# Three spacer tiles wider by 128 bytes: dense products whose operands and weights all begin at 64 modulo 256 bytes

## The chip, the core and the metric

The kernel runs on one NeuronCore of a Trainium2 chip. The metric is the device time of one execution in microseconds (us). Times of several executions are given as a median with the lowest and the highest; the profile is of one further execution.

## What is computed

A two-layer encoder trunk over 1280 tokens of 1024 channels, float32. The tokens are two batches that share the weights: a prompt of 256 and a sample of 1024. Layer 0 mixes tokens with a bidirectional RWKV-7 recurrence, layer 1 with neighbourhood attention; after each mixer comes a squared-ReLU MLP.

```python
for layer in range(DEPTH):                       # 2
    h = _rms_norm(x, p['norm_mix_g'][layer])
    y = rwkv7_mixer(h, ...) if layer == 0 else neighbourhood_attention(h, ...)
    x = x + y                                    # y ends in "@ w_o", 1024 x 1024
    h = _rms_norm(x, p['norm_mlp_g'][layer])
    x = x + jnp.square(jax.nn.relu(h @ w_up[layer])) @ w_down[layer]   # 1024 -> 4096 -> 1024
```

## The kernel before

Activations lie channels by tokens: 8 blocks (`k`, `KT = 8`) of 128 channels on the 128 partitions, the tokens along the free dimension. The tokens come in three segments, `SEGS = [(0, 256), (256, 768), (768, 1280)]`: `s = 0` is the prompt, `s = 1, 2` are the sample, 512 columns each.

**Dense products.** A float32 operand is split into two `float32r` tiles, a high part and a low rest (`wsplit`, L93 to L104, for weights: ACT copies the high part, L102, another engine subtracts, L103). `mm3` (L106 to L110) then makes three TensorE products into one PSUM bank: high weights with high operand (L108), high weights with low operand (L109), low weights with high operand (L110). The weights are the stationary operand, 128 x 128, loaded before each product; the activations are the moving operand, 256 or 512 columns of 4 bytes.

**The two channel layers.** `channel_layer` (L1349 on) runs once for each layer: the mixer's output product with the residual, then the MLP. Its operand is `self.act`, made by `act_tiles` (L1223) in the pool `actp`: for each `k` a high and a low tile of the prompt (`ahp`, `alp`, 256 columns) and of the sample (`ahs`, `als`, 1024 columns). `dense` (L1385) runs over the 8 `k`, 24 matmuls for one bank. In the MLP the hidden layer has 32 blocks `f`. `up(f, s)` is one `dense` with the weights `whi`, `wlo` from the pool `clw`, then ReLU (L1439, ACT), square (L1440, POOL), and the split into `hh`, `hl` (L1442 ACT, L1443 DVE) in the pool `clh`. `down([f], s)` multiplies `hh`, `hl` with the weights of block `f` from the pool `cld`, 8 output blocks `m` of three matmuls each, and DVE adds each bank to `x` (L1461). The loop interleaves them: `up(f, 0)`, `down(f-1, 0)`, `up(f, 1)`, `down(f-1, 1)`, `up(f, 2)`, `down(f-1, 2)`. The order of the instructions is that of the code; the down products of the last two blocks come together at the end, in an order fixed by `manual_schedule`.

Between the layers `attention` runs with an order written out by hand for TensorE: query and key projections (`qk_proj`, weights in the pool `atw`, operand `self.act`), eight pairs of heads, scores, softmax, transposes against the identity in `cst`, values. Ahead of layer 0's channel layer `gated` makes the gate product (`sgh`, `sgl`, `sgs` with `gh`, `gl`, `gs`, four matmuls to a bank, the fourth with 96 rows) from tiles in the pool `gp`, which `gate_begin` opens while the recurrence is still running, together with layer 0's `clk` and `clw`. In the first part of the kernel the key projection multiplies `mh`, `ml` with `whi`, `wlo` (pools `mixp`, `wpA`), and the receptance product `rps` multiplies `mh`, `ml` with `wh`, `wl`.

**Where tiles lie.** Pools of the left side are stacked upward from the low end of a partition, in the order in which they are opened, those of the right side downward from the high end; inside a pool the tiles follow each other upward. So a tile's start is the sum of what lies before it. Some tiles in the code hold nothing: the ones named `space`, `space0`, `space1` only move what is laid behind them. Starts of the dense products' operands in the kernel before, in bytes modulo 256 (all columns and blocks that a product addresses begin a multiple of 256 bytes further, so the remainder holds for each of its reads):

| product | moving operand | start mod 256 | weights | start mod 256 |
|---|---|---|---|---|
| layer 0 output, up (sample) | `ahs`, `als` | 192 | `clw` | 192 |
| layer 0 down (sample) | `hh`, `hl` | 64 | `cld` | 192 |
| layer 1 output, up (sample) | `ahs`, `als` | 192 | `clw`, `atw` | 64 |
| layer 1 down (sample) | `hh`, `hl` | 64 | `cld` | 192 |
| query, key (sample) | `ahs`, `als` | 192 | `atw` | 64 |
| output, up, query, key (prompt) | `ahp`, `alp` | 96 | as the sample's | |
| down (prompt) | `hh`, `hl` | 224 | `cld` | 192 |
| gate product | `sgh`, `sgl`, `sgs` | 192 | `gp` | 192 |
| key projection of layer 0 | `mh`, `ml` | 64 | `wpA` | 64 |
| receptance product of layer 0 | `mh`, `ml` | 64 | `wh`, `wl` | 64 |

Modulo 512, `ahs` lies at 448, layer 0's `clw` at 192, layer 1's at 320, `hh` at 64, `cld` at 448, the gate's tiles at 192, `mh` at 64, `wpA` at 320, `wh` at 64.

Of the kernel before, what the change touches and what calls it, by code (L numbers as in the profile page):

```python
# [5 lines left out]
F32 = mybir.dt.float32  # L6
# [7 lines left out]
P = 128  # L14
# [47 lines left out]
class Trunk:  # L62
# [748 lines left out]
    def at(self, t, f, level=3):  # L811
        self.todo.append((t, len(self.todo), f, level))
# [410 lines left out]
    def act_tiles(self, pool):  # L1223
        
        def tiles(part, n):
            return [[pool.tile([P, n], F32R, name=f"{x}{part}{k}") for x in ("ah", "al")] for k in range(KT)]
        prompt = tiles("p", TP)
        pool.tile([P, 24], F32, name="space")
        sample = tiles("s", T - TP)
        return [tuple(Parts(p, s) for p, s in zip(prompt[k], sample[k])) for k in range(KT)]  # L1230

# [47 lines left out]
    def gate_begin(self):  # L1279


        nc, tc = self.nc, self.tc
        at = lambda t, f, *x: self.at(16.0 * (len(self.jobs) - 1) + t, lambda: f(*x))

        def begin():
            self.ectx.close()
            self.clctx, self.gctx = ExitStack(), ExitStack()
            pool = lambda c, name, bufs: c.enter_context(tc.tile_pool(name=name, bufs=bufs, reuse_waits="tile", side="right"))
            self.clk, self.clw = pool(self.clctx, "clk", 2), pool(self.clctx, "clw", 2)
            gp = self.gp = pool(self.gctx, "gp", 1)  # L1290
            self.gate = [[gp.tile([P if i < 2 else 96, n], F32R, name=nm + "hls"[i]) for i in range(3)] for nm, n in (("sg", T), ("g", 1024))]
            gp.tile([P, 512], F32, name="graw", tag="graw", bufs=7)
            self.wo = []

        def load(src, c0, c1, stacked):
            raw = self.gp.tile([P, 512], F32, name="graw", tag="graw", bufs=7)
            raw = raw[:, :c1 - c0]
            if stacked:
                for j in range(3):
                    nc.sync.dma_start(raw[32 * j:32 * j + 32], src[P:P + 32, c0:c1])  # L1300
            else:
                nc.sync.dma_start(raw, src[:P, c0:c1])
            self.graws.append(raw)

        def cut(i, c0, c1, stacked):
            raw = self.graws.pop(0)
            hi, lo, st = (z[:, c0:c1] for z in self.gate[i])
            if stacked:
                low = slice(32, 64) if i else slice(64, 96)
                nc.scalar.copy(st, raw[:96])  # L1310
                nc.gpsimd.tensor_tensor(out=st[low], in0=raw[low], in1=st[low].bitcast(F32), op=ALU.subtract)
            else:
                nc.scalar.copy(hi, raw)
                nc.gpsimd.tensor_tensor(out=lo, in0=raw, in1=hi.bitcast(F32), op=ALU.subtract)

        def weight(m):
            self.wo.append(self.wsplit(self.clw, self.a["w_o"][m], 1024, nc.gpsimd, tag="u"))
        self.graws = []
        at(2.0, begin)
        parts = [(i, c0, min(c0 + 512, n), st) for i, n in ((0, T), (1, 1024)) for st in (0, 1) for c0 in range(0, n, 512)]  # L1320
        for k, (i, c0, c1, st) in enumerate(parts):
            src = self.a["g2"] if i else self.scr["sg2_d"]
            t = 7.0 + 0.9 * k
            at(t - 2.0, load, src, c0, c1, st)
            at(t, cut, i, c0, c1, st)
        at(16.5, weight, 0)
        at(17.5, weight, 1)
# [21 lines left out]
    def channel_layer(self, layer, x_src, src, wname, dst, gnext=None, gate=False):  # L1349
# [6 lines left out]
        with ExitStack() as ctx:  # L1356
            pool = lambda name, side="left": ctx.enter_context(tc.tile_pool(name=name, bufs=2, reuse_waits="tile", side=side))
# [19 lines left out]
            wd_, wh_ = pool("cld"), pool("clh")  # L1377
            wh_.tile([P, 8], F32, name="space0", bufs=1)
            for t in ("hh", "hl"):
                wh_.tile([P, TP], F32R, name=t, tag=t + "False", bufs=2)  # L1380
            wh_.tile([P, 24], F32, name="space1", bufs=1)
            ones = xp.tile([P, P], F32, name="ones", bufs=1)
            nc.gpsimd.memset(ones, 1.0)

# [615 lines left out]
```

## Time and profile before

| | |
|---|---|
| median of 3 runs | 4114.17 us (4107.8 to 4115.26) |
| the profiled execution | 4116.18 us |
| its span, first to last instruction | 4114.4 us |
| mean granted TensorE clock | 0.961 of full speed |
| DMA | 393.22 MB, mean 96 GB/s |

The engines are PE (TensorE's matmuls), PEld (its loads of weights, beside the matmuls), DVE, ACT, POOL and SP, whose queue issues most DMAs. The row of an engine in the slices gives its busy share in each of 40 equal parts of the span, in tenths. A row of a group reads: line, engine, operation, output and inputs by the program's names with buffer numbers left out, shapes, count, then busy time and mean duration of one, then the time that the engine stood idle just before. A row of the timeline begins with the start of an instruction and its duration, both in us. The ends of matmuls are modelled and overlap, so that the pace of a stream is read from start to start.

In the span, layer 0's channel layer takes about 1424 to 2500 us with its MLP from about 1558 on, the attention about 2580 to 3095 us, layer 1's channel layer the rest, with its MLP from about 3230 on.

### The profile page before, as it was taken

Reading aid. Unit: us, or ns where it says so; the run is one execution under the profiler, and the core shown is the slowest. Engines: PE = TensorE matmul, PEld = TensorE weight load, DVE = VectorE, ACT = ScalarE, POOL = GpSimd, SP = SyncE. Lnnn points to the kernel's source line nnn. Section 1 sums busy time; section 2 is a strip of 40 time slices with the busy share of each in tenths; the row PEclk is TensorE's granted clock in tenths of the full one; section 3 lists DMA queues with packets and bytes.
Section 4 is the critical chain, followed back from the end, with each engine's and each line's share of the span. In section 5 each row is a group of like instructions: output and inputs, shape, how many; then the busy total and the mean of one; then the engine's idle time right before and its main releaser. Section 6 shows DMA issues by size and latency. Waiting matters only on the chain.

```text
span 4114.4 us, 86971 instructions
## 1 busy us (share of the span) xinstructions
PE 3820.9 (93%) x35188; PEld 3211.4 (78%) x35188; DVE 2465.9 (60%) x4771; ACT 1544.5 (38%) x3731; POOL 1284.7 (31%) x1238
## 2 busy tenths in 40 slices
PE   7888979688889799999999999999989999999999
PEld 4665659678888688888888879777758788888888
DVE  7898972466666447555555571466774755555555
ACT  6776752345455441111111132455663211111111
POOL 4450001123323534222222250445553422222222
PEclk8997889799999899999999999999999999999999
DMA  3326655866765331111111115243344111101101
GB/s 109 90 85 216 210 190 151 207 171 176 179 173 141 118 123 31 36 42 42 32 41 42 36 65 179 75 92 77 78 108 134 48 34 42 42 31 42 42 31 62
DMA packets 384001, 393.22 MB, mean 96 GB/s; under 512 B 161872, under 2 KB 306480, under 8 KB 382320
## 3 DMA queue, kind: packets, MB, share of 16 engines
q1 hardware_dynamic: 327728, 307.82, 26.7%
q10 hardware_dynamic: 46704, 61.35, 4.4%
q0 software_dynamic: 9168, 18.49, 1.7%
q8 instruction: 276, 4.52, 0.5%
q14 instruction: 125, 1.02, 0.1%
HBM read 277.54 MB, written 121.24 MB: 97 GB/s over the span
## 4 chain that ended last, share of the span: by engine, by line
PE 73%; DVE 12%; issue 5%; DMA 4%; ACT 3%; POOL 2%; SPq 0%; ACTq 0%; DVEq 0%; POOLq 0%
PE ps L108 18%; PE ps L110 17%; PE ps L109 17%; PE bx L1017 3%; PE by L1017 3%; PE kps L979 2%; PE vps L530 1%; PE vps L531 1%; PE vps L532 1%; PE op L1914 1%; PE zps L1185 1%; PE aps L852 1%; PE yps L941 1%; PE pt L1856 1%; DVE mu L199 1%
## 5 line engine op out<-in xcount | busy, mean ns | idle before, releaser
L1461 DVE TENSOR_TENSOR x<-ps,x 128x256 f32<-128x256 f32 x1488 | 815.2, 594 | 638.6 <-PE ps L110 637.2
L103 POOL TENSOR_TENSOR wlo<-raw,whi 128x1024 fp32r<-128x1024 f32 (+1 forms) x178 | 391.1, 2197 | 873.9 <-ACT whi L102 873.9
L108 PE MATMUL ps<-ahs,whi 128*128 128x512 f32 x1536 | 616.4, 401 | 0.0
L110 PE MATMUL ps<-ahs,wlo 128*128 128x512 f32 x1536 | 603.7, 393 | 0.0
L109 PE MATMUL ps<-als,whi 128*128 128x512 f32 x1536 | 603.2, 393 | 0.0
L108 PE MATMUL ps<-hh,whi 128*128 128x512 f32 (+1 forms) x1536 | 550.5, 358 | 11.9 <-DVE x L1461 11.8
L110 PE MATMUL ps<-hh,wlo 128*128 128x512 f32 (+1 forms) x1536 | 550.3, 358 | 0.0
L109 PE MATMUL ps<-hl,whi 128*128 128x512 f32 (+1 forms) x1536 | 550.1, 358 | 0.0
L102 ACT CAST whi<-raw 128x1024 fp32r<-128x1024 f32 (+1 forms) x206 | 200.9, 975 | 711.8 <-PE ps L109 655.6
L108 PEld LDWEIGHTS ps<-ahs,whi 128*128 128x128 f32 x1536 | 289.5, 188 | 65.2 <-issue 6.8
L110 PEld LDWEIGHTS ps<-ahs,wlo 128*128 128x128 f32 x1536 | 289.0, 188 | 64.7
L108 PEld LDWEIGHTS ps<-hh,whi 128*128 128x128 f32 x1536 | 290.5, 189 | 60.2 <-DVE x L1461 14.8
L109 PEld LDWEIGHTS ps<-als,whi 128*128 128x128 f32 x1536 | 289.6, 189 | 57.1 <-issue 1.0
L1440 POOL TENSOR_TENSOR rl<-rl 128x512 f32<-128x512 f32 (+1 forms) x192 | 174.4, 908 | 494.9 <-PE ps L110 454.9
L110 PEld LDWEIGHTS ps<-hh,wlo 128*128 128x128 f32 x1536 | 290.4, 189 | 46.3
L109 PEld LDWEIGHTS ps<-hl,whi 128*128 128x128 f32 x1536 | 290.4, 189 | 46.0
L1439 ACT ACTIVATE rl<-ps 128x512 f32<-128x512 f32 (+1 forms) x192 | 100.6, 524 | 538.9 <-PE ps L110 538.9
L984 DVE TENSOR_TENSOR zz<-kps,cst 128x512 f32<-128x512 f32 x160 | 110.4, 690 | 209.5 <-ACT ll L989 209.4
L1442 ACT CAST hh<-rl 128x512 fp32r<-128x512 f32 (+1 forms) x192 | 105.6, 550 | 321.1 <-POOL rl L1440 321.0
L108 PE MATMUL ps<-ahp,whi 128*128 128x256 f32 x768 | 222.9, 290 | 0.2 <-DVE ot L1344 0.2
L110 PE MATMUL ps<-ahp,wlo 128*128 128x256 f32 x768 | 216.0, 281 | 0.5 <-POOL wlo L103 0.5
L109 PE MATMUL ps<-alp,whi 128*128 128x256 f32 x768 | 215.9, 281 | 0.0
(341 smaller groups left out, 8699.7 us busy)
## 6 DMA issues: line engine op xcount, KB each, us to landing
x<-x_d SPq DMA_DIRECT2D x88, 512.0 KB, 5.9
raw<-in_w_down_dram SPq DMA_DIRECT2D x64, 512.0 KB, 3.5
raw<-in_w_up_dram SPq DMA_DIRECT2D x64, 512.0 KB, 3.5
eab<-x_d SPq DMA_DIRECT2D x80, 256.0 KB, 5.0
x_d<-ar ACTq DMA_DIRECT2D x32, 512.0 KB, 2.8
x_d<-bk ACTq DMA_DIRECT2D x32, 512.0 KB, 3.9
bs<-tab SPq DMA_DIRECT2D x128, 96.0 KB, 4.4
v_d<-vt ACTq DMA_DIRECT2D x80, 128.0 KB, 3.3
```

Source lines behind the costliest of these rows:

```text
L102: nc.scalar.copy(hi[:, cs], raw)
L103: lo_eng.tensor_tensor(out=lo[:, cs], in0=raw, in1=hi[:, cs].bitcast(F32), op=ALU.subtract)
L108: mm(ps, sh, mh, start=first, stop=False)
L109: mm(ps, sh, ml, start=False, stop=False)
L110: mm(ps, sl, mh, start=False, stop=last)
L979: mm(J["kp"][out, e, 192 * c + 192 - w:192 * c + 192], x[es, b, 2 * pr + c], x[es, 5 - w // 64:5, 2 * pr + c], start=True, stop=True)
L984: nc.vector.tensor_tensor(out=z, in0=src[:, :, :, :P], in1=self.mask[d].unsqueeze(1).unsqueeze(1).to_broadcast([P, 2, 2, P]), op=ALU.mult)
L1017: mm = lambda out, a, b, start, stop: nc.tensor.matmul(out, a, b, start=start, stop=stop, skip_group_check=True)
L1439: nc.scalar.activation(r[:, :n], ps[:, :n], AF.Relu)
L1440: nc.gpsimd.tensor_tensor(out=r[:, :n], in0=r[:, :n], in1=r[:, :n], op=ALU.mult)
L1442: nc.scalar.copy(hh[:, :n], r[:, :n])
L1461: nc.vector.tensor_tensor(out=xv, in0=ps[:, :n], in1=xv, op=ALU.add)
```

## The change

No instruction is added, removed or moved. Three tiles that nothing reads or writes change in size, each by 32 float32 columns, 128 bytes in a partition:

```diff
@@ act_tiles
         prompt = tiles("p", TP)
-        pool.tile([P, 24], F32, name="space")
+        pool.tile([P, 56], F32, name="space")
         sample = tiles("s", T - TP)
@@ gate_begin
             self.clk, self.clw = pool(self.clctx, "clk", 2), pool(self.clctx, "clw", 2)
+            self.clk.tile([P, 32], F32, name="space", bufs=1)
             gp = self.gp = pool(self.gctx, "gp", 1)
@@ channel_layer
                 wh_.tile([P, TP], F32R, name=t, tag=t + "False", bufs=2)
-            wh_.tile([P, 24], F32, name="space1", bufs=1)
+            wh_.tile([P, 56], F32, name="space1", bufs=1)
```

The first lies in `actp` between the prompt's and the sample's tiles: it moves `ahs`, `als` and every left pool that is opened later (`xp`, `cld`, `clh`, the attention's) up by 128. The second is new and is the first tile of layer 0's `clk`, the pool at the high end of the right side: it makes that pool longer, so that `clw` and `gp`, which are stacked below it, move down by 128, while the other tiles of `clk` stay. Layer 1 opens its own `clk` and `clw`, without a space; they stay where they are. The third lies in `clh` between the prompt's and the sample's hidden tiles; with the shift of the pool, the sample's `hh`, `hl` move up by 256 and the prompt's by 128. The table above then reads, for the products that the change touches:

| product | moving operand, mod 256 | weights, mod 256 |
|---|---|---|
| layer 0 output, up (sample) | 64 | 64 |
| layer 0 down (sample) | 64 | 64 |
| layer 1 output, up (sample) | 64 | 64 |
| layer 1 down (sample) | 64 | 64 |
| query, key (sample) | 64 | 64 |
| output, up, query, key (prompt) | 96 | 64 |
| down (prompt) | 96 | 64 |
| gate product | 64 | 64 |

Modulo 512 the pairs are: layer 0 output and up 64 and 64, layer 1 up 64 and 320, down 320 and 64.

## The prediction

> **What bounds the kernel now.** I read the page first: busy shares, slices, the costliest groups.
>
> ```profile
> span 4114.4 us, 86971 instructions
> ...
> PE 3820.9 (93%) x35188; PEld 3211.4 (78%) x35188; DVE 2465.9 (60%) x4771; ACT 1544.5 (38%) x3731; POOL 1284.7 (31%) x1238
> ...
> PE   7888979688889799999999999999989999999999
> ...
> PEclk8997889799999899999999999999999999999999
> ...
> L110 PE MATMUL ps<-ahs,wlo 128*128 128x512 f32 x1536 | 603.7, 393 | 0.0
> L109 PE MATMUL ps<-als,whi 128*128 128x512 f32 x1536 | 603.2, 393 | 0.0
> ```
>
> PE carries 93% of the span. From the fifteenth slice on it is full in all but one, with the granted clock at 90% or more, and the dense products stand there with no idle time before them. The next question is whether anything but PE decides inside the two channel layers, so I took the table of stretches, 800 us from each layer's MLP.
>
> ```profile
> 1600.00:2400.00 800.00, 800.00 (x4147) 681.89 (x4145) 422.00 (x773) 151.18 (x231) 215.08 (x145) 1.00 0.12 38
> 3270.00:4070.00 800.00, 800.00 (x4123) 678.69 (x4122) 422.80 (x774) 149.25 (x229) 211.63 (x143) 1.00 0.12 36
> ```
>
> The columns are stretch, length, then busy time and instructions of PE, PEld, DVE, ACT, POOL, then clock, DMA share and GB/s. PE is busy for all 800 us in both; the next engine, DVE, for 422. So each matmul that starts sooner shortens the run by as much. Clock and load of every other engine agree to about 4 us, yet layer 0 gets through 4147 matmuls where layer 1 gets through 4123. The groups by shape say which ones (layer 0's two rows first, then layer 1's):
>
> ```profile
> L110 PE MATMUL ps<-hh,wlo 128*128 128x512 f32 x461 | 182.1, 395 | 0.0
> L110 PE MATMUL ps<-ahs,wlo 128*128 128x512 f32 x466 | 181.8, 390 | 0.0
> ...
> L110 PE MATMUL ps<-hh,wlo 128*128 128x512 f32 x464 | 183.1, 395 | 0.0
> L110 PE MATMUL ps<-ahs,wlo 128*128 128x512 f32 x456 | 179.9, 395 | 0.0
> ```
>
> The up product on `ahs` takes 390 ns in layer 0 and 395 in layer 1; the down product on `hh` 395 in both. These are durations with modelled ends; what counts is the distance from start to start, which the timeline has. Below are first rows of whole groups of 24 matmuls (8 k or m, 3 products each): layer 0 up, the same group six matmuls later, down, what follows; then layer 1 up, down, what follows.
>
> ```profile
> 1713.76 0.39 PE L108 MATMUL ps<-ahs,whi 128*128 128x512 f32 x1
> ...
> 1715.13 0.39 PE L108 MATMUL ps<-ahs,whi 128*128 128x512 f32 x1
> ...
> 1719.21 0.40 PE L108 MATMUL ps<-hh,whi 128*128 128x512 f32 x1
> ...
> 1724.81 0.28 PE L108 MATMUL ps<-ahp,whi 128*128 128x256 f32 x1
> ...
> 3514.97 0.39 PE L108 MATMUL ps<-ahs,whi 128*128 128x512 f32 x1
> ...
> 3520.54 0.39 PE L108 MATMUL ps<-hh,whi 128*128 128x512 f32 x1
> ...
> 3526.12 0.39 PE L108 MATMUL ps<-ahs,whi 128*128 128x512 f32 x1
> ```
>
> Start to start, each group over 24: layer 0 up 5.45 us, 227.1 ns; layer 0 down 5.60 us, 233.3 ns; layer 1 up 5.57 us, 232.1 ns; layer 1 down 5.58 us, 232.5 ns. Inside the fast group the first six take 228.3 ns each and the other 18 take 4.08 us, 226.7 ns each: it settles.
>
> **What sets the fast cadence apart.** With the allocator's byte offsets (table ahead), moving operand and weights modulo 256: layer 0 up 192 and 192, fast; layer 1 up 192 and 64, slow; down 64 and 192, slow in both layers. Layer 0 up and layer 1 up are the same code on the same `ahs` tiles beside the same load; their weights lie 128 bytes elsewhere. So neither the 192 of the moving operand nor the 192 of the weights makes a stream fast: they must be equal modulo 256. The change wants both at 64, so the row that matters most is a stream with 64 and 64. There is one, the key projection, uninterrupted for twelve matmuls:
>
> ```profile
> 258.22 0.39 PE L110 MATMUL ps<-mh,wlo 128*128 128x512 f32 x1
> ...
> 260.94 0.39 PE L110 MATMUL ps<-mh,wlo 128*128 128x512 f32 x1
> ```
>
> 2.72 us for twelve is 226.7 ns each, the settled value again.
>
> **The change, part by part.** It adds and removes no instruction; the three tiles are never written. It only moves addresses.
>
> *Layer 0 down.* `hh`, `hl` go from 64 to 64 (128 from `actp`, 128 from their own space), the weights in `cld` from 192 to 64. 32 blocks x 2 sample segments x 24 are 1536 matmuls, from 233.3 to the 227.1 of the fast group with its settling: 6.2 ns each, -9.5 us.
>
> *Layer 1 output product and up.* `ahs`, `als` go from 192 to 64; the weights stay at 64. 8 x 2 x 24 and 1536 make 1920 matmuls, 232.1 to 227.1: -9.6 us.
>
> *Layer 1 down.* As in layer 0: 1536 matmuls, 232.5 to 227.1, -8.3 us.
>
> *Layer 0 output product and up.* Both operands go from 192 to 64, so 1920 matmuls stay at 227.1. Cost 0, and this is where the third space is needed: without it the weights stay at 192 and these take the 232.1 of the unequal pair.
>
> *Query and key projections of the attention.* 768 sample matmuls go from 192 against 64 to 64 against 64, at most 768 x 5.0 = 3.8 us. But here they come in threes among scores and transposes, so that six in a row to settle are rare, and PE is not always the one that is late:
>
> ```profile
> 2640.00:3095.00 455.00, 417.96 (x2847) 318.66 (x2846) 317.90 (x774) 272.93 (x722) 245.26 (x278) 0.97 0.38 87
> ...
> PE op L1914 <- DVE ot L1915: 8.4, 2, 6.9
> PE s L1838 <- DVE s L1873: 8.3, 4, 5.3
> ```
>
> 418 of 455 us busy, and waits for DVE. I take -0.5, between 0 and -3.8.
>
> *Prompt products* (256 columns). Moving 96 or 224 against weights at 192 or 64 become 96 against 64 everywhere. Both layers show the same mean for a pair that the change leaves as it is (layer 1) and one that it makes the same (layer 0):
>
> ```profile
> L108 PE MATMUL ps<-ahp,whi 128*128 128x256 f32 x232 | 64.9, 280 | 0.0
> ...
> L108 PE MATMUL ps<-ahp,whi 128*128 128x256 f32 x231 | 64.6, 280 | 0.0
> ```
>
> Cost 0, within 1 us.
>
> *The rest of what moves.* The tiles of attention on the left side all shift by 128: scores, values, `ks` and `qs` together, so their distances to each other stay; the transposes against the identity at 128 go from 64 above to 64 below. 5 ns on the 416 of them (8 head pairs x 52) bounds it at 2 us either way; taken as 0. On the other engines the 128 bytes do nothing: `rl` lies at 192 in layer 0 and at 64 in layer 1, and POOL squares it in
>
> ```profile
> L1440 POOL TENSOR_TENSOR rl<-rl 128x512 f32<-128x512 f32 x58 | 60.6, 1045 | 225.9 <-PE ps L110 220.9 <-ACT rl L1439 5.1
> ...
> L1440 POOL TENSOR_TENSOR rl<-rl 128x512 f32<-128x512 f32 x58 | 60.6, 1045 | 242.1 <-PE ps L110 225.4 <-ACT rl L1439 16.7
> ```
>
> 1045 ns both times. Where a pool opens over an older one, shifted tiles may touch another tile and wait for it; such openings come a few times in the run, and 3.3 us, the longest wait that a dense product has now, bounds each:
>
> ```profile
> PE ps L108 <- DVE x L1461: 11.8, 6, 3.3
> ```
>
> Taken as 0, 3 us to the bad side kept for the range. What is late next when PE runs 2% faster in these streams: nothing near, DVE has 378 of 800 us free.
>
> *Sum.* -9.5 - 9.6 - 8.3 - 0.5 = -27.9 us. The profiled execution took 4116.18 us (span 4114.4 and 1.8 around it) and would take 4088.3; it lies 2.0 above the median of the runs, so that from 4114.17 I get 4086.3, in round numbers 4086.
>
> The Trainium skill, "TensorE: Matmul & The Clock Gate", section "Step-by-step: what each phase is for", speaks against all this: TensorE reads the moving operand and the weights through two independent SBUF ports, and loading the next weights takes no bandwidth from the running matmul. By it no start address would matter and the sum would be 0. The 227.1 and 232.1 of the same product in two layers do not agree with it as far as I can read them.
>
> **Rivals.**
>
> *No change (4114).* The two reads never meet, and the difference between the layers has a cause that is not in the addresses. Then all 6912 sample matmuls keep their cadence. For it: the two slow down products, at the same addresses in both layers, are not equal (233.3 and 232.5), so that history counts too. Against it: the even load in the table of stretches, and the key projection at 226.7.
>
> *A period of 512 bytes (4098).* Modulo 512 the fast pairs of now lie 256 apart (`ahs` 448 on weights 192; `mh` 64 on weights 320). Layer 0's up product would come to 64 on 64, distance 0. The gate product is at distance 0 today, 192 on 192, and is slow:
>
> ```profile
> 1414.77 0.40 PE L108 MATMUL ps<-sgh,gh 128*128 128x512 f32 x1
> ...
> 1418.50 0.40 PE L108 MATMUL ps<-sgh,gh 128*128 128x512 f32 x1
> ```
>
> Sixteen in 3.73 us are 233.1 ns. That would cost 1920 x 6.0 = 11.5 us and leave -16. Against it: every fourth matmul there has 96 rows, which may break the settling; and a receptance stream at 64 on 64 modulo 512 ends its groups fast:
>
> ```profile
> 442.02 0.39 PE L109 MATMUL rps<-ml,wh 128*128 128x512 f32 x1
> ...
> 442.93 0.39 PE L110 MATMUL rps<-mh,wl 128*128 128x512 f32 x1
> ```
>
> four in 0.91 us, 227 ns. The same price would show if the third space did not move the weights of layer 0.
>
> *Slower: 64 itself is the slow start (4124).* All the slow channel streams have one operand at 64, the only fast one has none. If a read that starts at 64 cannot settle, layer 0's output and up products go from 227.1 to the 232.5 of layer 1's down, 1920 x 5.4 = +10.4 us, and nothing else gains. It decides at 64 against 64 in a long stream. Against it stand the twelve of the key projection, and they are few.
>
> **How the numbers follow.** Forecast, equal modulo 256 is what counts, 0.78; a period of 512 or a third space without effect, 0.09; no change 0.07; 64 slow 0.05; 0.01 is left for waits that eat the gain. About 0.2% (8 us) is what a measurement of this kernel can tell from no change. Forecast and the 512 case (-16 us, 0.4%) are faster, 0.87; same 0.08; slower 0.05. Range: if everything settles at 226.7, the 4992 improved matmuls and the 1920 others give another 0.4 ns each, 2.8 us, and the projections up to 3.3 more, hence 4080, and 3 for the transposes and the spread of a median: 4077. Upward the 512 case with the 3 us of waits: 4101.
>
> **What would show it.** In the profile after: the 512-wide rows on `ahs` and `hh` in both layers at 389 or 390 ns, groups of 24 in 5.45 us or less; the 800 us stretches with some 4190 to 4200 matmuls each; the prompt rows at 280; DVE, ACT and POOL means as now. The forecast is wrong if layer 0's `ahs` rows rise to 395 (the 512 period, or 64 itself if the others stay), if layer 1's stay at 395, or if new idle time stands before L108.

## The result and the profile after

The kernel with the change takes 4083.11 us (median of 6 runs, 4077.62 to 4087.64), the kernel before beside it 4111.86 (6 runs, 4101.26 to 4115.26). The ratio is 0.9932, with a 95% interval from 0.9918 to 0.9947: 0.7% faster. Forecast were 4086, in a range from 4077 to 4101. Of the 3 us between 4086 and the result, 2.3 are the starting point, 4111.86 in place of the 4114.17 that the forecast began with: it expected a gain of 28, and 28.75 came. The interval of the ratio, worked out on 4111.86, reaches from 22 to 34 us, so that part of this closeness is luck. A line above L1290 keeps its number in the new profile; below, the added line moves all by one (L1461 is L1462, L1440 is L1441).

The span and the busy time of the engines, from the page of the changed kernel:

```profile
span 4083.1 us, 86970 instructions
...
PE 3783.9 (93%) x35188; PEld 3201.4 (78%) x35188; DVE 2463.5 (60%) x4771; ACT 1545.7 (38%) x3731; POOL 1285.2 (31%) x1238
```

The span is 31.3 us shorter and PE is busy for 37.0 us less with the same 35188 matmuls; DVE, ACT and POOL stay within 2.4 us. The same two stretches of 800 us, one in each layer's MLP:

```profile
1600.00:2400.00 800.00, 800.00 (x4199) 689.62 (x4198) 424.00 (x778) 154.53 (x236) 217.29 (x147) 1.00 0.12 38
3270.00:4070.00 800.00, 800.00 (x4214) 690.24 (x4214) 430.51 (x792) 149.96 (x231) 217.67 (x149) 1.00 0.13 40
```

PE is still busy throughout, with 4199 and 4214 matmuls where it had 4147 and 4123. And the groups of TensorE by shape, layer 0's two rows (1600 to 2400 us), then layer 1's (3270 to 4050 us, so that its counts are not those of the 800 us before):

```profile
L110 PE MATMUL ps<-ahs,wlo 128*128 128x512 f32 x475 | 184.8, 389 | 0.0
L110 PE MATMUL ps<-hh,wlo 128*128 128x512 f32 x464 | 180.5, 389 | 0.0
...
L110 PE MATMUL ps<-ahs,wlo 128*128 128x512 f32 x463 | 180.1, 389 | 0.0
L110 PE MATMUL ps<-hh,wlo 128*128 128x512 f32 x449 | 174.7, 389 | 0.0
```

All four are at 389 ns; three of them stood at 395. The timeline shows the pace itself. First rows of an up group that follows the prompt's products, of the same group six matmuls on, of the down group after it, and of the next up group:

```profile
1705.43 0.39 PE L108 MATMUL ps<-ahs,whi 128*128 128x512 f32 x1
...
1706.82 0.39 PE L108 MATMUL ps<-ahs,whi 128*128 128x512 f32 x1
...
1710.90 0.39 PE L108 MATMUL ps<-hh,whi 128*128 128x512 f32 x1
...
1716.34 0.39 PE L108 MATMUL ps<-ahs,whi 128*128 128x512 f32 x1
```

The first six take 1.39 us, 231.7 ns each; the next 18 take 4.08 us, 226.7 each; the down group takes 5.44 us for 24, 226.7 in the mean. Averaged by place in the group over all groups of layer 0's MLP, the up group behind the prompt's products has its first five distances at 231.5 ns and 226.7 from the sixth on; the up group behind a down group and every down group have 226.7 from their first matmul on. So in this kernel a settled stream hands its pace to the next stream of equal starts, and the prompt's 256-column products in between upset it.

Where the 31.3 us of the span come from is read from the first row of each layer's down products and the last row of its MLP (for layer 0, the first value product behind it). Before:

```profile
1559.35 0.28 PE L108 MATMUL ps<-hh,whi 128*128 128x256 f32 x1
...
2443.29 0.28 PE L530 MATMUL vps<-whi,ahp 128*128 128x256 f32 x1
...
3231.39 0.28 PE L108 MATMUL ps<-hh,whi 128*128 128x256 f32 x1
...
4109.28 0.40 PE L110 MATMUL ps<-hh,wlo 128*128 128x512 f32 x1
```

After:

```profile
1563.64 0.28 PE L108 MATMUL ps<-hh,whi 128*128 128x256 f32 x1
...
2437.27 0.41 PE L530 MATMUL vps<-whi,ahp 128*128 128x256 f32 x1
...
3217.19 0.28 PE L108 MATMUL ps<-hh,whi 128*128 128x256 f32 x1
...
4077.98 0.39 PE L110 MATMUL ps<-hh,wlo 128*128 128x512 f32 x1
```

Layer 0's MLP went from 883.94 to 873.63 us (-10.3), layer 1's from 877.89 to 860.79 (-17.1). What lies between them, the attention and layer 1's output product, went from 788.10 to 779.92 (-8.2), and the stretch ahead of 1559 us became 4.3 longer. Whether these last two are the change's is taken up under "Why the prediction was right".

### The profile page after: what moved, and what is told of

It is laid out like the page before. It is cut to its first block, busy times and chain, and to the rows that moved or that the text cites. A ratio compares the mean times of both kernels' runs of the same rounds, so it can differ in the third digit from the quotient of the medians.

```text
span 4083.1 us, 86970 instructions
## 1 busy us (share of the span) xinstructions
PE 3783.9 (93%) x35188; PEld 3201.4 (78%) x35188; DVE 2463.5 (60%) x4771; ACT 1545.7 (38%) x3731; POOL 1285.2 (31%) x1238
## 4 chain that ended last, share of the span: by engine, by line
PE 73%; DVE 12%; issue 5%; DMA 4%; ACT 4%; POOL 2%; SPq 0%; ACTq 0%; DVEq 0%; POOLq 0%
PE ps L108 17%; PE ps L109 17%; PE ps L110 17%; PE bx L1017 3%; PE by L1017 3%; PE kps L979 2%; PE vps L530 1%; PE vps L531 1%; PE vps L532 1%; PE zps L1185 1%; PE aps L852 1%; PE op L1915 1%; PE yps L941 1%; DVE mu L199 1%; DVE cs L646 1%
## 5 line engine op out<-in xcount | busy, mean ns | idle before, releaser
L1462 DVE TENSOR_TENSOR x<-ps,x 128x256 f32<-128x256 f32 x1488 | 813.0, 596 | 607.6 <-PE ps L110 607.6
L110 PE MATMUL ps<-ahs,wlo 128*128 128x512 f32 x1536 | 598.9, 390 | 0.0
L110 PE MATMUL ps<-hh,wlo 128*128 128x512 f32 (+1 forms) x1536 | 543.1, 354 | 0.0
L110 PEld LDWEIGHTS ps<-ahs,wlo 128*128 128x128 f32 x1536 | 288.3, 188 | 61.7
L1441 POOL TENSOR_TENSOR rl<-rl 128x512 f32<-128x512 f32 (+1 forms) x192 | 174.9, 911 | 489.5 <-PE ps L110 450.2
L110 PEld LDWEIGHTS ps<-hh,wlo 128*128 128x128 f32 x1536 | 289.9, 189 | 40.5
L1440 ACT ACTIVATE rl<-ps 128x512 f32<-128x512 f32 (+1 forms) x192 | 100.8, 525 | 532.3 <-PE ps L110 532.3
L110 PE MATMUL ps<-ahp,wlo 128*128 128x256 f32 x768 | 215.6, 281 | 1.3 <-POOL wlo L103 1.3
```

What stands on the lines that cost most here:

```text
L110: mm(ps, sl, mh, start=False, stop=last)
L1440: nc.scalar.activation(r[:, :n], ps[:, :n], AF.Relu)
L1441: nc.gpsimd.tensor_tensor(out=r[:, :n], in0=r[:, :n], in1=r[:, :n], op=ALU.mult)
L1462: nc.vector.tensor_tensor(out=xv, in0=ps[:, :n], in1=xv, op=ALU.add)
```

## The experiments

To compare streams, one number is formed for each from all its rows: the mean distance from the start of a 512-column matmul to the start of the next instruction, over all distances between 220 and 245 ns. Before, it was 227.3 (layer 0, `ahs`), 233.0 (layer 0, `hh`), 232.3 and 232.4 (layer 1, `ahs` and `hh`); after, 227.3, 226.8, 227.2 and 226.7. "Distance of starts" below is the start of the moving operand less that of its weights, modulo 256.

**One part undone.**

```diff
             self.clk, self.clw = pool(self.clctx, "clk", 2), pool(self.clctx, "clw", 2)
-            self.clk.tile([P, 32], F32, name="space", bufs=1)
```

> The change without its new space in layer 0's clk: layer 0's output and up products go back to weights at 192 against an operand at 64, all else as in the change. If equal starts modulo 256 are what lets a stream settle, these 1920 matmuls come at 232 ns instead of 227, layer 0's ahs rows read 394 or 395 ns, and about 9.5 us of the 28 are lost: some 19 us faster than before. If the distance did not matter, and only the operands' own place at 64 did, layer 0's up would stay at 227 and nothing be lost.

4088.84 us, ratio 0.9952 (0.9936 to 0.9968). Groups by shape in layer 0, 1600 to 2400 us:

```profile
L110 PE MATMUL ps<-ahs,wlo 128*128 128x512 f32 x470 | 185.8, 395 | 0.0
L110 PE MATMUL ps<-hh,wlo 128*128 128x512 f32 x458 | 179.0, 391 | 0.0
```

Layer 0's up product is back at 395 ns (mean distance 232.5), and its output product with it; its down product keeps nearly all (227.3; its first three distances behind each up group are 228.6 to 229.8). The operand's own start is 64 here as in the change, so that the start by itself is not what gains. From the first output product to the first value product behind the MLP, layer 0 takes 9.5 us more than in the change (1016.83 against 1007.34), the 9.5 that the third space was expected to be worth.

**Equal at 192 in place of 64, and equal modulo 512 in layer 1.**

```diff
-        pool.tile([P, 56], F32, name="space")
+        pool.tile([P, 24], F32, name="space")
...
-            self.clk.tile([P, 32], F32, name="space", bufs=1)
...
                 wk, wp = pool("clk", "right"), pool("clw", "right")
+                wk.tile([P, 96], F32, name="space", bufs=1)
...
-            wh_.tile([P, 56], F32, name="space1", bufs=1)
+            wh_.tile([P, (56, 120)[layer]], F32, name="space1", bufs=1)
```

> All sample operands and weights of the channel layers begin at 192 instead of 64, equal again; the projections of the attention alone stay unequal (192 against 64). In layer 1 the pairs are also equal modulo 512, in layer 0 they lie 256 apart there. If equality modulo 256 is what counts, all four streams run at 226.7 to 227.3 ns and the time is within 3 us of the change's, less whatever the attention gained by its own pairs (0.5 to 4 us). If 64 is a good start in itself, the streams fall back to 232 and the time to that of before. If 512 is the period, layer 1's two streams fall back (about 18 us lost).

4082.16 us, ratio 0.9943 (0.9926 to 0.9959). Layer 0's two rows, then layer 1's:

```profile
L109 PE MATMUL ps<-als,whi 128*128 128x512 f32 x464 | 180.5, 389 | 0.0
L109 PE MATMUL ps<-hl,whi 128*128 128x512 f32 x464 | 180.5, 389 | 0.0
...
L109 PE MATMUL ps<-als,whi 128*128 128x512 f32 x457 | 177.7, 389 | 0.0
L109 PE MATMUL ps<-hl,whi 128*128 128x512 f32 x452 | 175.8, 389 | 0.0
```

The other two products on `ahs`, `als` stand at 390 and 391 ns in both layers, because the up group behind the prompt takes ten matmuls to settle here, where the change takes five. Mean distances 227.5, 226.8, 227.5, 226.7. Equality modulo 256 does it, at 192 as at 64, with pairs 256 apart modulo 512 (layer 0) and equal modulo 512 (layer 1). The time is that of the change within what the intervals can tell.

**Other distances.** Three kernels set each layer's distance of starts by the spaces alone; the diff of the first, and the sizes in the others.

```diff
-            self.clk.tile([P, 32], F32, name="space", bufs=1)
+            self.clk.tile([P, 40], F32, name="space", bufs=1)
...
                 wk, wp = pool("clk", "right"), pool("clw", "right")
+                wk.tile([P, 16], F32, name="space", bufs=1)
...
-            wh_.tile([P, 56], F32, name="space1", bufs=1)
+            wh_.tile([P, (64, 72)[layer]], F32, name="space1", bufs=1)
```

> The change with the moving operand 32 bytes above its weights in layer 0 (output, up and down) and 64 above in layer 1. If only equal starts settle, all four streams run at about 232 ns and the time is that of before. If it is the distance of 128 alone that disturbs, all four stay at 227. A third case: the prompt's products, whose operand lies 32 above the weights, settle at 116.7 ns for 256 columns, 10.0 over 256 cycles at 2.4 GHz, where pairs at equal starts take 120.0; if that carries over to 512 columns, layer 0's streams come at 223.3 and layer 0 gains another 11 us.

Second (24, 24 and 48, 80 columns in the same places):

> The same with the moving operand 32 bytes below its weights in layer 0 and 96 above in layer 1. Only equal starts settle: about 232 ns in all four streams, the time of before. Only 128 disturbs: 227 in all four. If the order of the two reads matters, layer 0 here differs from layer 0 with the operand 32 above.

Third (16, 40 and 40, 32 columns):

> The change with the moving operand 64 bytes below its weights in layer 0 and 96 below in layer 1. The runs with 32, 64 and 96 above and 32 below gave 233, 229.3, 233.2 and 233 ns, 128 gave 232 to 233. If the distance counts whichever way it goes, layer 0 comes at 229.3 and layer 1 at 233.2. If it is a distance around a circle of 256 in one direction, 64 below is 192 above, which no run has had, and may be anything from 226.7 to 233.

One run each: 4106.36, 4111.39 and 4108.53 us; the kernel before had 4107.16 beside the first two and 4108.13 beside the third. Mean distances from start to start, up and down:

| distance of starts | 0 | +32 | +64 | +96 | 128 | -96 | -64 | -32 |
|---|---|---|---|---|---|---|---|---|
| output and up, ns | 227.2 | 233.1 | 229.2 | 233.1 | 232.3 | 233.8 | 233.1 | 233.1 |
| down, ns | 226.7 | 233.4 | 229.6 | 233.2 | 232.4 | 234.0 | 233.0 | 233.2 |

(0 and 128 are layer 1 after and before.) Each distance other than 0 and 128 was run in one layer only, and two layers can differ by 0.6 ns at the same addresses (the down products before: 233.0 and 232.4), so that differences of that size in the table say nothing. Of the eight distances only 0 settles at 226.7. The third case, that 512 columns might gain at 32 above as 256 columns do, fell. It also matters which of the two starts is the higher one: 64 above costs 2.0 to 2.9 ns over equal starts, 64 below about 6. At +64 the three products of layer 1 differ: from start to start the first takes 231.2 ns, the second 226.8, the third 229.8. Their rows (first, third, second):

```profile
L108 PE MATMUL ps<-ahs,whi 128*128 128x512 f32 x453 | 178.6, 394 | 0.0
L110 PE MATMUL ps<-ahs,wlo 128*128 128x512 f32 x452 | 177.7, 393 | 0.0
...
L109 PE MATMUL ps<-als,whi 128*128 128x512 f32 x452 | 176.0, 389 | 0.0
```

**Which reads meet.**

```diff
         hi = pool.tile([P, n], F32R, name="whi", tag=tag + "h", bufs=hb)
+        if tag == "u":
+            pool.tile([P, 32], F32, name="space2", bufs=1)
         lo = pool.tile([P, n], F32R, name="wlo", tag=tag + "l", bufs=hb)
...
-            self.clk.tile([P, 32], F32, name="space", bufs=1)
```

> Which two reads of TensorE have to be at equal starts. In the pool clw 32 columns stand between the high and the low weights: in layer 0 the low weights alone lie 128 bytes away from the operand (192 against 64), in layer 1 the high weights alone (the low ones are equal); the down products stay equal, as a control at 226.8. If a matmul's stream meets the load of the next weights, in layer 0 only the product during which the low weights are loaded is late (L109), in layer 1 the two others. If it meets its own weights, it is L110 in layer 0 and L108 and L109 in layer 1. Either way layer 0's up comes at a third of the loss, some 228.7 ns, and layer 1's at two thirds, 230.5; if one unequal pair in three is enough to keep the stream from settling, both come at 231 or more.

4101.27 us in one run (before 4108.13). Layer 0, where only the low weights are 128 bytes away; lines are two higher here, so that L110, L111, L112 are the first, second and third product. The last row is the control, the down product:

```profile
L112 PE MATMUL ps<-ahs,wlo 128*128 128x512 f32 x466 | 184.6, 396 | 0.0
L111 PE MATMUL ps<-als,whi 128*128 128x512 f32 x465 | 184.0, 396 | 0.0
L110 PE MATMUL ps<-ahs,whi 128*128 128x512 f32 x465 | 181.3, 390 | 0.0
...
L112 PE MATMUL ps<-hh,wlo 128*128 128x512 f32 x456 | 177.4, 389 | 0.0
```

Neither of the two single pairs holds. The first product, whose own weights and next weights are both equal, keeps 390 ns; the second, during which the low weights are loaded, and the third, which uses them, are both at 396. From start to start the three take 227.4, 232.4 and 233.7 ns. The mean is 231.2 ns, and 233.0 in layer 1, where each product has high weights as its own or as the next ones and all three rows stand at 394 to 396. That is the expectation's last case: one unequal load in three is enough to keep the stream from 226.7, and here two matmuls pay for it.

**The change once more, and two attempts beyond it.** The first attempt shifts the value weights' pool:

```diff
+                vp.tile([P, 8], F32, name="space", bufs=1)
                 vp.tile([P, 256], F32, name="vt", tag="vt", bufs=2)
```

> The change, and a space of 8 columns ahead of the tiles of the value weights in the attention's first part, so that these products of 256 columns (240 groups of three) have the moving operand 32 bytes above the stationary one, as the prompt's dense products have, instead of at equal starts. If 256 columns do best at a distance of 32 (the prompt settles at 116.7 there, and the run in which its starts were equal gave 120.0), the value products go from 120.0 to about 117 ns, 2.4 us less in the stretch of the value blocks; the total is then that of the change within what can be told. If equal starts are best at any width, they go the other way.

The second moves the prompt's operands and the value weights:

```diff
+        pool.tile([P, 40], F32, name="space3")
         prompt = tiles("p", TP)
-        pool.tile([P, 56], F32, name="space")
+        pool.tile([P, 16], F32, name="space")
...
-            wh_.tile([P, 8], F32, name="space0", bufs=1)
+            wh_.tile([P, 48], F32, name="space0", bufs=1)
...
-            wh_.tile([P, 56], F32, name="space1", bufs=1)
+            wh_.tile([P, 16], F32, name="space1", bufs=1)
...
+                vp.tile([P, 48], F32, name="space", bufs=1)
                 vp.tile([P, 256], F32, name="vt", tag="vt", bufs=2)
```

> The change, with the prompt's operands moved to start 64 bytes below their weights (0 against 64) in place of 32 above, and the moving operand of the attention's value products 64 below the sample's stationary one; the sample's products stay at equal starts. In the run with 64 and 96 below, layer 1's prompt products happened to stand 64 below and took 113.8 ns on average, settling at 113, 113, 114, against 116.7 in the change. If the best distance depends on the width (0 for 512 columns, 64 below for 256), the 3456 prompt matmuls of the channel layers come at 113.4 to 114 (10 to 11 us less) and the value products with the sample at 113.4 instead of 120 (3.8 us less): about 4068 to 4070 where the change has 4083. If that pace came from the unsettled neighbours in that run, the prompt stays at 116 to 120 and the time is the change's or up to 12 us over it; the sample's streams stay at 226.7 to 227.3 either way.

> The change itself once more, on the same chip as the run before, to have both beside the same runs of the kernel before: a ratio within 0.992 to 0.995, the four sample streams at 226.7 to 227.3 ns. The attention's main part took 477 to 484 us in the profiles so far, with equal and unequal projections alike, and should again lie there, if the 6.6 us that it was shorter in the first profile of the change are chance.

The change again: 4079.84 us, ratio 0.9919 (0.9903 to 0.9935), streams at 227.3, 226.8, 227.2 and 226.7 ns. With the value weights 32 above: 4076.15, ratio 0.9920 (0.9907 to 0.9932); the value products with the sample came down from 119.9 to 116.8 ns in the mean, as expected, worth less than can be told. With the prompt 64 below: 4077.4, ratio 0.9911 (0.9894 to 0.9929), not told apart from the change either, and its expectation fell: the prompt's products took 117.7 ns, not 113.4. The sample's up groups behind the prompt, though, are at 226.7 from their first matmul on in this kernel, so that all four sample streams have a mean of 226.7. What failed is the idea that a distance has one pace. The value products of that kernel show two, at the same addresses modulo 256; three matmuls in a row early and nine later:

```profile
2500.11 0.28 PE L532 MATMUL vps<-vh,als 128*128 128x256 f32 x1
...
2500.45 0.28 PE L532 MATMUL vps<-vh,als 128*128 128x256 f32 x1
...
2520.25 0.28 PE L530 MATMUL vps<-vh,ahs 128*128 128x256 f32 x1
...
2521.31 0.28 PE L530 MATMUL vps<-vh,ahs 128*128 128x256 f32 x1
```

0.34 us for three are 113 ns each, 1.06 us for nine 117.8. The addresses being the same, something that came before must decide which of the two a stream falls into; what it is was not found.

## Why the prediction was right

**Layer 0 down, -9.5 forecast.** 1536 matmuls from 233.0 to 226.8 ns are -9.5. The price came from one group of each kind, and the whole layer bears it out.

**Layer 1 output and up, -9.6; down, -8.3.** From 232.3 to 227.2 is -9.8; from 232.4 to 226.7 is -8.8. The down term was a little too small, for one reason: the forecast gave every group the 227.1 of a group with its settling, but a down group behind a settled up group has nothing to settle. The same holds for layer 0, where the sampled slow group (233.3) stood a little above the mean and hid it.

**Layer 0 output and up, 0.** 227.3 before and after, with the third space; 232.5 without it. So the three spaces are one edit, and the run without the third loses what the forecast said.

**Prompt, 0 within 1 us.** Slightly wrong: layer 0's prompt products went from 117.7 to 116.8 ns, 1.5 us over 1728 of them. The rows of the groups, rounded to a nanosecond, could not tell this (the first product: 280 in both layers before, 279 in both after).

**Attention, -0.5, and no new waits.** The projections' matmuls came from 232.5 to 230.5 ns, so that most did not settle, as forecast; 2 ns on 768 are 1.5 us, three times the term. That they come in threes was misread: in the profile before, 41 stretches have three in a row, 70 have six and 18 have nine, and six are about what a group needs to settle. From the first scores to the last product with the values the attention took 483.8 us before, 477.3 after and 481.4 in the change's second profile, and between 479.4 and 483.7 in the eight other kernels, with equal and unequal projections alike (479.4 is the one with unequal ones). So the bulk of the 8.2 us seen there in the first pair is not shown to be the change's, and an effect of 2 or 3 us could not be seen. The same goes for the stretch ahead of layer 0: the gate product began at 1398.9 us before, and at 1403.2 and 1393.7 in two profiles of the changed kernel, which is one and the same program. The span fell by 31.3 us and the medians by 28.75, since the profiled execution before lay 4.3 us above its median and the one after 1.8.

**The rivals.** No change: fallen, the same products changed pace with their addresses alone. The Trainium skill says that loading the next weights takes no bandwidth from the running matmul ("TensorE: Matmul & The Clock Gate", "Step-by-step: what each phase is for"). Taken as the prediction took it, that no start address matters, it does not agree with these traces: 227 against 232 to 234 ns. Whether it is bandwidth that an unequal pair costs, no run shows. A period of 512: fallen, layer 0's up product at 64 on 64 modulo 512 holds 227.3, and layer 1 at 448 on 448 modulo 512 holds 227.5. The slow gate product was the misleading row. It has equal starts before and after, 192 and then 64, and the change did not move it: sixteen in 3.73 us, 233.1 ns, both times. After:

```profile
1420.56 0.40 PE L108 MATMUL ps<-sgh,gh 128*128 128x512 f32 x1
...
1424.29 0.40 PE L108 MATMUL ps<-sgh,gh 128*128 128x512 f32 x1
```

Its fourth matmul, with 96 rows, sets it apart from the streams that settle; that this is the cause was not tried. 64 as a slow start: fallen, and 192 is not a fast one by itself either (232.3 ns in layer 1 before).

What stays open is why: the runs show that equal starts modulo 256 of the two operands that TensorE reads let a stream settle at 226.7 ns, and in which matmuls an unequal one is paid, not what the two reads contend for, if they do. Unequal streams are not irregular: averaged by place in the group, layer 0's down products before alternate between 229 and 237.5 ns, and layer 1's down products repeat a pattern of seven between 228 and 241, at the same addresses even modulo 512. So more than the addresses decides which pattern an unequal stream falls into.

## What to carry to other kernels

Where TensorE is busy without a gap, compare the same product in two places of the program from start to start; a difference of 2% under equal load can be the address of a tile, and a few hundred unused bytes (here 384 in a partition) can set it right. For streams of 512 columns in float32r, put the moving operand and its weights at the same start modulo 256, for high and low parts alike, since one unequal load in three already undoes most of it. Common starts of 64 and 192 were run, no others, and the gate product stays at 233 ns with either. Do not carry the rule over to another width: 256 columns did no better at equal starts (119.9 ns, the value products with the sample) than 32 apart (116.8), and at one and the same distance they showed more than one pace.

## What the runs showed of the hardware

A stream of 512-column matmuls with equal starts modulo 256 settles at 226.7 ns, and a following stream of equal starts takes this over at once. How many matmuls it takes depends on what ran before: behind the prompt's products five in the change, ten with all starts at 192, none with the prompt 64 below its weights. The cost over 512 columns depends on the distance of starts and its sign: 0 settles at 226.7, 64 above has a mean of 229.2 to 229.6, the others that were run 232 to 234 ns. At 256 columns and 64 below, two settled paces, 113 and 117.7 ns, came in one and the same run.
